# One pair of seven products more in the first half of the two long down linears, with its weight sums made in the mixer

## The chip, the cores and the metric

The kernel runs on one core of a Trainium2 chip. The metric is device microseconds of one execution (a lower number is faster). Of the engines, TensorE (PE in the profile) multiplies, VectorE (DVE) and ScalarE (ACT) prepare its operands and take its results, GpSimd (POOL) and SyncE (SP) issue transfers.

## What is computed

One decoder layer on 256 positions and 16 learned ones put ahead of them, in float32: a SwiGLU network, a mixer (differential attention beside a short gated convolution, merged by gates), a second SwiGLU network, each added to the residual, and a final norm. Cut to what matters here:

```python
D_MODEL, SEQ, N_META, D_FF = 2048, 256, 16, 5632     # D_FF = ((8 * D_MODEL // 3 + 255) // 256) * 256

def swiglu_ffn(h, w_gu, w_down):
    gate, up = jnp.split(h @ w_gu, 2, axis=-1)
    return (jax.nn.silu(gate) * up) @ w_down

s = s + 0.5 * swiglu_ffn(rms_norm(s, norm_ffn1), ffn1_w_gu, ffn1_w_down)
h = rms_norm(s, norm_mix)
q, k, v, b_gate, c_gate, u = jnp.split(h @ w_in, splits, axis=-1)
...                                # attention of q, k, v; convolution of b_gate, c_gate, u; merge
s = s + 0.5 * swiglu_ffn(rms_norm(s, norm_ffn2), ffn2_w_gu, ffn2_w_down)
```

The change lies in the last `@ w_down`; the preparation of its data lies in `h @ w_in`, in the parts k, v, c_gate and u.

## The kernel before

A float32 operand is held as a high and a low part (`wh` and `wl` of a weight: ScalarE casts the high part, VectorE subtracts it from the weight for the low one). One product of two operands is three matmuls into one bank of PSUM: high by high, low by high, high by low.

The second network works on 256 rows as two blocks of 128, in three parts of its hidden width. Two of the parts have 16 chunks of 128 hidden rows: these are the long down linears, each with a first half (`u == 0`, 1024 of the 2048 output columns) and a second. `linear_mix` takes the chunks by pairs. With two row blocks and two column groups of 512, a pair is a 2 x 2 by 2 x 2 block product, and has one of three kinds:

- D: eight products, from two weight tiles of 128x1024.
- S: seven products (a Winograd form of Strassen's scheme), from weight tiles that include four sums of weights. VectorE makes the sums in the linear itself, into the tiles `t13` and `t24` (lines 705, 706, 707).
- P: the same seven products, with the sums read from DRAM (line 693 for `t24`, line 694 for `t13`, 512 KB each, on SP's queue) and three of the four weight blocks (768 KB in place of 1024).

`t13` and `t24` of these linears are the two buffers with the tag "tt". A plan names, by position, the kinds of its pairs, the places at which left-over work of the linear's start is put in, which sums of activations are made when, and the order of the pairs. Eight pairs of seven products each would be 56 products; the plan `DOWN_FIRST` before has six D and two S, so 6 x 8 + 2 x 7 = 62. Sums of the activations (`sp`, ScalarE and VectorE, `sum_of_parts`) are put into the linear by the list `side`, one entry at the end of each pair.

The sums that P pairs read are made earlier, by pieces of half a pair (class `Making`): fetch 512 KB into a tile `mk`, three additions on VectorE, store 512 KB to DRAM (line 339). Most are made in the first network. Five pairs, ten pieces, are made in the mixer by `tick_later`, called once a chunk while v, k, c and u are computed: its step i adds up and stores piece i - 1 and fetches piece i, into the two "tt" buffers in turn. All of these fetches and stores are on GpSimd's queue before.

Around them, in v to u, run the attention steps: TensorE computes scores, VectorE scales them and takes the maximum (lines 960, 964), ScalarE the exponential (line 967), VectorE normalises and takes the difference (lines 971 to 975), TensorE transposes it (`aT`, line 984), ScalarE copies it out (`aB`). Each engine and each queue takes its instructions in the order in which they stand: one that waits holds those behind it.

Of the kernel before, what the change touches and what calls it, by code (L numbers as in the profile page):

```python
# [16 lines left out]
D = 2048  # L17
# [3 lines left out]
F = 5632  # L21
DC = D // P
GC = 4
GW = GC * P
W2 = D // 2
# [12 lines left out]
N_AUX = 3  # L38
# [12 lines left out]
FFN2_MORE = ("DPPPDSPP", (2,), {(4, 1): 5}, ())  # L51
OUT_FIRST = ("DDSDSDSD", (1,), {(1, 1): 2, (3, 1): 4, (5, 1): 6}, ())
OUT = ("DDDDSDSD", (), {(3, 1): 4, (5, 1): 6}, ())
DOWN_FIRST = ("DDDDSDSD", (1,), {(3, 1): 4, (5, 1): 6}, ())
DOWN = ("DDSDSDSD", (), {(1, 1): 2, (3, 1): 4, (5, 1): 6}, ())
DOWN_LAST = ("DDDSDS", (1,), {(2, 1): 3, (4, 1): 5}, ())
AHEAD = 3
# [1 line left out]
TICK_COUNT = 512  # L59
# [11 lines left out]
MADE = [(0, d, p) for d, plan in enumerate(GATE_UNITS) for p, kind in enumerate(plan[0]) if kind == "P"]  # L71
MADE += [(1, u, p) for u in range(F // GW) for p, kind in enumerate(_unit_plan(u)[0]) if kind == "P"]
MADE_LATER = [(0, 0, 1), (0, 0, 3), (1, 1, 5), (1, 2, 1), (1, 3, 1)]
MADE = [m for m in MADE if m not in MADE_LATER]
LATER_TICKS = (TICK_COUNT + 16, TICK_COUNT + 124)


@with_exitstack
def decoder_layer(ctx: ExitStack, tc: tile.TileContext, t, out):
    nc = tc.nc  # L80
# [52 lines left out]
    def load_vectors():  # L133
# [7 lines left out]
        out=mask[:, T - P :],  # L141
        in_=mask[:, T - P :],
# [150 lines left out]
    spare, ticks, last_wl, last_store, last_sum = [], [], [], [], []  # L293
    last_load, ahead_of_split = [], []
    side = []
# [15 lines left out]
        while ahead:  # L311
            ahead.pop(0)[0]()

    made = [[{} for _ in range(n)] for n in (D // GW, F // GW, 2)]

    class Making:

# [1 line left out]
        def __init__(self, n, unit, p, k):  # L319
            self.n, self.unit, self.p, self.k = n, unit, p, k  # L320

        def fetch(self, i, first):
            self.t = early_tile(i)
            if first:
                with tc.issue_after(last_wl[0]):
                    nc.vector.memset(self.t[:, 0, 0:1], 0.0)
            nc.gpsimd.dma_start(out=self.t, in_=t["ffn2_made_of"][self.n, self.k])

        def add(self):
            v = self.t  # L330
# [10 lines left out]
    for n, (f, u, p) in enumerate(MADE):  # L341
        spare.extend(Making(n, made[f][u], p, k) for k in range(2))
    spare_later = [
        Making(len(MADE) + n, made[f][u], p, k) for n, (f, u, p) in enumerate(MADE_LATER) for k in range(2)
    ]

    def tick_later(n):
        n0, n1 = LATER_TICKS
        steps = len(spare_later) + 1
        i = (n - n0) * steps // (n1 - n0)  # L350
        if not n0 <= n < n1 or (n > n0 and i == (n - 1 - n0) * steps // (n1 - n0)):
            return
        if i:
            with tc.issue_after(last_wl[0]):
                spare_later[i - 1].add()
            spare_later[i - 1].store()
        if i < len(spare_later):
            with tc.issue_after(last_store[0]):
                spare_later[i].fetch(N_AUX + i % 2, i < 2)

    def tick():
        ticks.append(0)
# [503 lines left out]
    w_in, w_qb, w_gate, w_out = t["w_in"], t["w_qb"], t["w_gate"], t["w_out"]  # L866
# [182 lines left out]
    for g in range(2):  # L1049
# [7 lines left out]
        if g == 0:  # L1057
# [13 lines left out]
            half = len(units) // 2  # L1071
# [57 lines left out]
    for d in range(D // GW):  # L1129
# [28 lines left out]
        if d < 2:  # L1158
            n = 3 * d
# [39 lines left out]
                out=lo, in0=src, scalar=gain, in1=hi.bitcast(F32), op0=ALU.mult, op1=ALU.subtract  # L1199
            )  # L1200

    def add_mix(plan, a, w, k0, u, by, adds, end):


        v = [[sT[i][u][:, q * GW : (q + 1) * GW] for q in range(2)] for i in range(2)]
        ev = {}

        def scaled(ps, out_, other, op1=ALU.add, by=by):
            nc.vector.scalar_tensor_tensor(out=out_, in0=ps, scalar=by, in1=other, op0=ALU.mult, op1=op1)

        late = []

        def add(out_, in_):
            if adds == "dma":
                late.append(lambda: nc.gpsimd.dma_start(out=out_, in_=in_, accum_op=ALU.add))
            elif adds == "side":
                late.append(lambda: nc.vector.tensor_add(out_, out_, in_))
            else:
                nc.vector.tensor_add(out_, out_, in_)

        def finish_adds():
            if adds == "side":
                side.extend(lambda fs=late[k : k + 2]: [f() for f in fs] for k in (0, 2))
            else:
                for f in late:
                    f()
            end()

        def done(k, ps):
            if k == "1":  # L1230
                ev["a"], ev["b"] = wide([P, 2, GW], "dpa"), wide([P, 2, GW], "dpb")
                nc.scalar.mul(ev["a"][:, 0, :], ps, by)
                add(v[0][0], ev["a"][:, 0, :])
            elif k in "56":
                if k == "6":
                    scaled(ps, ev["a"][:, 1, :], ev["a"][:, 0, :])
                    add(v[1][0], ev["a"][:, 1, :])
                else:
                    ev["p5"] = ps
                if "p5" in ev and (k == "6" or "6" in ev):  # L1240
                    scaled(ev["p5"], ev["b"][:, 0, :], ev["a"][:, 1, :], ALU.subtract)
                    for i in range(2):
                        add(v[i][1], ev["b"][:, 0, :])
            elif k == "7":
                scaled(ps, v[1][0], v[1][0])
                scaled(ps, v[1][1], v[1][1], by=-by)
            else:
                i, q = {"2": (0, 0), "3": (0, 1), "4": (1, 0), "x": (1, 1)}[k]
                scaled(ps, v[i][q], v[i][q])
            ev[k] = True  # L1250
            if all(n in ev for n in "1234567x"):
                pending.append(finish_adds)

        linear_mix(plan, a, w[u], "pd", done, k0)

    def out_done(u):
        def f():
# [58 lines left out]
    w_gu, w_down, w_last = t["ffn2_w_gu"], t["ffn2_w_down"], t["ffn2_w_down_last"]  # L1316
    thirds = [list(range(0, 4)), list(range(4, 8)), list(range(8, ng))]
    for half in thirds:
# [7 lines left out]
        if final:  # L1326
            for q in range(2):
                nc.gpsimd.dma_start(
                    out=gfin[q],
                    in_=t["norm_final"][q * W2 : (q + 1) * W2].rearrange("(o d) -> o d", o=1).to_broadcast([P, W2]),  # L1330
                )
        ma = Mixed(m, 0, True)
        for u in range(2):
# [32 lines left out]
            if final and u == 0:  # L1366
                side.append(lambda: None)
                side.extend(lambda p=p: ma.sum_of_parts(p) for p in (3, 5))
                add_mix(
                    DOWN_LAST, ma, w_down, half[0] * GC, u, 0.5, "side",  # L1370
                    lambda score=score: side.extend(
                        lambda iq=iq: [score(*k) for k in iq] for iq in (((0, 0), (1, 0)), ((0, 1),), ((1, 1),))
                    ),
                )
            elif u == 0:
                side.extend([lambda: None] * 2)
                side.extend(lambda p=p: ma.sum_of_parts(p) for p in (4, 6))
                side.extend((lambda: None, lambda ma=ma: ma.sum_of_parts(2)))
                add_mix(DOWN_FIRST, ma, w_down, half[0] * GC, u, 0.5, "dma", lambda: None)
            elif not final:  # L1380
                add_mix(DOWN, ma, w_down, half[0] * GC, u, 0.5, "dma", lambda: None)
            else:
                linear_tok(ops, w_last, chunks, 0, "pd", down, hold=HOLD, side_at=(1, 2, 3, 4, 5))
# [22 lines left out]
def _laid_out(np, inputs):  # L1406
    a = {k: np.asarray(v) for k, v in inputs.items()}
# [7 lines left out]
    for name in ("ffn1_w_gu", "ffn1_w_down"):  # L1415
        w = a[name][0]
        d[name] = np.stack([_in_fours(w, c) for c in range(0, w.shape[1], GW)])
    w = a["w_in"][0]
# [3 lines left out]
    w = a["w_branch"][0]  # L1422
# [2 lines left out]
    )  # L1425
    d["w_out"] = np.stack([_in_pairs(np, a["w_out"][0], c, c + GW) for c in (0, W2)])
    d["ffn2_w_gu"] = np.stack([_in_pairs(np, a["ffn2_w_gu"][0], c, F + c) for c in range(0, F, GW)])
    ws = [(a["w_gate"][0], D, GW), (a["ffn2_w_gu"][0], F, GW), (a["w_out"][0], GW, W2)]
    d["ffn2_made_of"] = np.stack(
        [  # L1430
            np.stack([_quarter(*ws[f][:2], 2 * p * P, u * ws[f][2] + k * GW // 2, GW // 2) for k in range(2)])
# [38 lines left out]
```

## Time and profile before

| | us |
|---|---|
| runs | 2124.95 (median), 2124.93, 2126.96 |
| profiled execution | 2125.68 |
| its span, first to last instruction | 2123.9 |
| granted clock of TensorE, mean | 0.999 |
| VectorE busy | 1780.8 (84%) |
| ScalarE busy | 1151.4 (54%) |
| GpSimd busy | 164.6 (8%) |
| first long down linear, first half | 1599.98 to 1643.14 |
| the ten pieces made in the mixer | first fetch 896.32, last store 1066.62 |

Times in the trace count from the start of the span. A busy share is a mean over stages with different limits, so a stage is read from its own stretch. The second long down linear begins 245.5 us after the first, at 1845.50.

### The profile page before, as it was taken

What the parts mean: (1) busy time and instruction counts of PE and PEld (TensorE: products, weight loads), DVE (VectorE), ACT (ScalarE), POOL (GpSimd) and SP (SyncE); (2) the same over time, 40 slices, a digit from 0 to 9 for tenths busy, and PEclk for the clock granted to TensorE, in tenths of its full rate; (3) what the DMA queues carried; (4) which work ended last, traced back from release to release, by engine and by line L of the source; (5) the groups of instructions that cost most, each with busy time, mean ns of one, the idle gap of its engine ahead of it and who ended that gap; (6) DMA issues with size and microseconds to landing.
All of it is one profiled execution on the core that took longest, in us unless ns stands there. A gap on an engine that the chain in (4) does not pass through costs nothing.

```text
span 2123.9 us, 33643 instructions
## 1 busy us (share of the span) xinstructions
PE 2112.8 (99%) x13087; PEld 1910.0 (90%) x13087; DVE 1780.8 (84%) x2490; ACT 1151.4 (54%) x1453; POOL 164.6 (8%) x261
## 2 busy tenths in 40 slices
PE   9999999999999999999999999999999999999998
PEld 9999999999999998899998888887888888888887
DVE  8777776677777778978898899999999899998998
ACT  6434443343443445655456565567775567656765
POOL 0111111111121110000000000000000100000000
PEclk9999999999999999999999999999999999999999
DMA  7989999999899885665565665566885988779963
GB/s 301 338 318 330 343 339 330 330 326 337 328 328 335 299 303 195 205 225 199 209 221 200 233 212 192 199 226 238 319 298 193 289 314 305 258 230 313 320 239 139
DMA packets 111328, 576.47 MB, mean 271 GB/s; under 512 B 12992, under 2 KB 13376, under 8 KB 71104
## 3 DMA queue, kind: packets, MB, share of 16 engines
q1 hardware_dynamic: 74160, 444.66, 58.4%
q0 software_dynamic: 36576, 128.99, 17.5%
q8 instruction: 102, 1.67, 0.3%
q10 hardware_dynamic: 432, 0.67, 0.1%
q14 instruction: 58, 0.48, 0.1%
HBM read 506.11 MB, written 63.96 MB: 268 GB/s over the span
## 4 chain that ended last, share of the span: by engine, by line
PE 98%; ACT 0%; DVE 0%; DMA 0%; issue 0%; SPq 0%; ACTq 0%; DVEq 0%
PE pg L666 6%; PE pg L664 6%; PE pg L665 6%; PE pd L447 4%; PE pd L445 4%; PE pu L447 4%; PE pu L446 4%; PE pu L445 4%; PE pg L447 4%; PE pd L446 4%; PE pg L445 4%; PE pg L446 4%; PE pd L664 4%; PE pd L666 4%; PE pd L665 4%; PE g L666 2%
## 5 line engine op out<-in xcount | busy, mean ns | idle before, releaser
L429 ACT CAST wh<-st 128x1024 fp32r<-128x1024 f32 x320 | 335.4, 1049 | 474.3 <-PE pu L446 142.0
L434 DVE TENSOR_TENSOR wl<-st,wh 128x1024 fp32r<-128x1024 f32 x320 | 390.6, 1223 | 211.7 <-ACT wh L429 211.6
L552 DVE TENSOR_TENSOR wl<-st,wh 128x1024 fp32r<-128x1024 f32 (+1 forms) x424 | 453.6, 1085 | 47.4 <-ACT wh L551 43.1
L551 ACT CAST wh<-st 128x1024 fp32r<-128x1024 f32 (+1 forms) x424 | 386.6, 942 | 172.4 <-PE pdx L665 43.2
L551 ACT CAST wh<-t 128x1024 fp32r<-128x1024 f32 x214 | 224.6, 1053 | 204.3 <-DVE t L707 84.1
L552 DVE TENSOR_TENSOR wl<-t,wh 128x1024 fp32r<-128x1024 f32 x214 | 257.9, 1222 | 29.4 <-ACT wh L551 24.2
L447 PE MATMUL pd<-mh,wl 128*128 128x272 f32 x704 | 203.1, 288 | 0.0
L445 PE MATMUL pg<-h,wh 128*128 128x272 f32 x704 | 201.9, 287 | 1.1 <-ACT wh L429 1.1
L445 PE MATMUL pd<-mh,wh 128*128 128x272 f32 x704 | 202.2, 287 | 0.0
L445 PE MATMUL pu<-h,wh 128*128 128x272 f32 x704 | 201.9, 287 | 0.0
L447 PE MATMUL pu<-h,wl 128*128 128x272 f32 x704 | 201.7, 287 | 0.0
L446 PE MATMUL pu<-h,wh 128*128 128x272 f32 x704 | 201.7, 287 | 0.0
L446 PE MATMUL pg<-h,wh 128*128 128x272 f32 x704 | 201.7, 287 | 0.0
L447 PE MATMUL pg<-h,wl 128*128 128x272 f32 x704 | 200.9, 287 | 0.0
L446 PE MATMUL pd<-ml,wh 128*128 128x272 f32 x704 | 200.7, 285 | 0.0
L665 PE MATMUL pg<-wh,h 128*128 128x512 f32 x375 | 146.7, 391 | 0.0
L664 PE MATMUL pg<-wh,h 128*128 128x512 f32 x375 | 146.2, 390 | 0.0
L666 PE MATMUL pg<-wl,h 128*128 128x512 f32 x375 | 145.5, 389 | 0.0
L339 POOL DMA_DIRECT2D made<-mk x118 | 86.1, 729 | 755.1 <-DVE mk L333 605.7
L445 PEld LDWEIGHTS pg<-h,wh 128*128 128x128 f32 x704 | 132.8, 189 | 1.3 <-ACT wh L429 1.3
L446 PEld LDWEIGHTS pd<-ml,wh 128*128 128x128 f32 x704 | 133.5, 190 | 0.0
L446 PEld LDWEIGHTS pg<-h,wh 128*128 128x128 f32 x704 | 132.7, 188 | 0.2 <-DVE h L234 0.2
(392 smaller groups left out, 5101.3 us busy)
## 6 DMA issues: line engine op xcount, KB each, us to landing
st<-in_ffn_w_gu_dram SPq DMA_DIRECT2D x118, 1024.0 KB, 7.3
st<-in_ffn_w_down_dram SPq DMA_DIRECT2D x82, 1024.0 KB, 7.0
mk<-in_ffn_made_of_dram POOLq DMA_DIRECT2D x118, 512.0 KB, 8.3
made<-mk POOLq DMA_DIRECT2D x118, 512.0 KB, 6.4
t<-made SPq DMA_DIRECT2D x118, 512.0 KB, 5.8
st<-in_ffn_w_gu_dram SPq DMA_DIRECT2D x54, 768.0 KB, 6.0
st<-in_w_in_dram SPq DMA_DIRECT2D x32, 1024.0 KB, 5.3
st<-in_w_gate_dram SPq DMA_DIRECT2D x27, 1024.0 KB, 4.8
```

The costliest lines, as they stand in the source:

```text
L339: last_store[:] = [nc.gpsimd.dma_start(out=self.unit[self.p][:, :, cs], in_=self.t).ins]
L429: nc.scalar.copy(out=wh[:, :m, :], in_=sw)
L434: last_wl[:] = [nc.vector.tensor_sub(wl[:, :m, :], sw, wh[:, :m, :].bitcast(F32)).ins]
L445: nc.tensor.matmul(a, wh[:, i, f], act.part(c, 0, t0, t1), start=first, stop=False)
L446: nc.tensor.matmul(a, wh[:, i, f], act.part(c, 1, t0, t1), start=False, stop=False)
L447: nc.tensor.matmul(a, wl[:, i, f], act.part(c, 0, t0, t1), start=False, stop=last)
L551: part_last[:] = [nc.scalar.copy(out=wh, in_=src).ins]
L552: part_last.append(nc.vector.tensor_sub(wl, src, wh.bitcast(F32)).ins)
L664: nc.tensor.matmul(ps[k], hi, wh, start=first, stop=False)
L665: nc.tensor.matmul(ps[k], lo, wh, start=False, stop=False)
L666: nc.tensor.matmul(ps[k], hi, wl, start=False, stop=left[k] == 0)
```

## The change

```diff
-DOWN_FIRST = ("DDDDSDSD", (1,), {(3, 1): 4, (5, 1): 6}, ())
+DOWN_FIRST = ("DDDPDSDP", (1,), {(4, 1): 5}, (0, 1, 3, 4, 5, 6, 7, 2))
...
 MADE_LATER = [(0, 0, 1), (0, 0, 3), (1, 1, 5), (1, 2, 1), (1, 3, 1)]
+MADE_LATER += [(2, 0, k + p) for k in (0, 8) for p in (4, 2)]
...
-LATER_TICKS = (TICK_COUNT + 16, TICK_COUNT + 124)
+LATER_TICKS = (TICK_COUNT + 16, TICK_COUNT + 126)
...
-        def fetch(self, i, first):
+        def fetch(self, i, first, eng=nc.gpsimd):
...
-            nc.gpsimd.dma_start(out=self.t, in_=t["ffn2_made_of"][self.n, self.k])
+            eng.dma_start(out=self.t, in_=t["ffn2_made_of"][self.n, self.k])
...
         if i < len(spare_later):
-            with tc.issue_after(last_store[0]):
-                spare_later[i].fetch(N_AUX + i % 2, i < 2)
+            spare_later[i].fetch(N_AUX + i % 2, i < 2, nc.scalar)
...
-    def add_mix(plan, a, w, k0, u, by, adds, end):
+    def add_mix(plan, a, w, k0, u, by, adds, end, made=None):
...
-        linear_mix(plan, a, w[u], "pd", done, k0)
+        linear_mix(plan, a, w[u], "pd", done, k0, made, True)
...
             elif u == 0:
-                side.extend([lambda: None] * 2)
-                side.extend(lambda p=p: ma.sum_of_parts(p) for p in (4, 6))
-                side.extend((lambda: None, lambda ma=ma: ma.sum_of_parts(2)))
-                add_mix(DOWN_FIRST, ma, w_down, half[0] * GC, u, 0.5, "dma", lambda: None)
+                for p in (None, 4, None, 6, 2):
+                    side.append((lambda: None) if p is None else lambda ma=ma, p=p: ma.sum_of_parts(p))
+                k0 = half[0] * GC
+                ready = {p: made[2][u][k0 // 2 + p] for p in (2, 4)}
+                add_mix(DOWN_FIRST, ma, w_down, k0, u, 0.5, "dma", lambda: None, ready)
...
-    ws = [(a["w_gate"][0], D, GW), (a["ffn2_w_gu"][0], F, GW), (a["w_out"][0], GW, W2)]
+    ws = [(a["w_gate"][0], D, GW), (a["ffn2_w_gu"][0], F, GW), (a["ffn2_w_down"][0], GW, W2), (a["w_in"][0], GW, 3 * W2)]
```

The first half of each long down linear takes its pairs in the order 0 1 3 4 5 6 7 2; pairs 4 and 2 are P, pair 6 is S, the other five are D: 5 x 8 + 3 x 7 = 61 products. The sums for the four P pairs of the two linears are eight more pieces for `tick_later`, eighteen in all, in 110 ticks instead of 108. All eighteen are fetched on ScalarE's queue, without the order behind the last store; a fetch still waits until the store of the piece before it in its buffer has landed. From line 72 on, most line numbers of the changed kernel are larger by one.

In the order of the instructions this stands as follows. ScalarE, at the first attention step (names: `st` a weight as fetched, `vN` values, `mk` a piece, `sc` scores), before:

```order
L429 CAST wh<-st 128x1024 x4
L930 COPY vN_9114<-pv 128x512 x2
L429 CAST wh<-st 128x1024 x2
L967 ACT_TABLE_LOAD
L967 ACTIVATE sc,sm<-sc,mx 128x144 x2
L429 CAST wh<-st 128x1024
L988 COPY aB<-aT 128x128
```

and in the changed kernel:

```order
L429 CAST wh<-st 128x1024 x3
L328 DMA mk<-in_ffn_made_of_dram 128x1024
L429 CAST wh<-st 128x1024
L930 COPY vN_9114<-pv 128x512 x2
L429 CAST wh<-st 128x1024 x2
L328 DMA mk<-in_ffn_made_of_dram 128x1024
L967 ACT_TABLE_LOAD
L967 ACTIVATE sc,sm<-sc,mx 128x144 x2
L429 CAST wh<-st 128x1024
L988 COPY aB<-aT 128x128
L328 DMA mk<-in_ffn_made_of_dram 128x1024
L967 ACTIVATE sc,sm<-sc,mx 128x272 x2
```

Fetches now stand among ScalarE's casts, exponentials and copies; the second one shown, the sixth of the eighteen, is directly ahead of the table load of the first exponential.

VectorE at the same place, before:

```order
L434 TENSOR_TENSOR wl<-st,wh 128x1024
L960 SCALAR_TENSOR_TENSOR sc<-sc_ps,rq,mask 128x144 x2
L434 TENSOR_TENSOR wl<-st,wh 128x1024
L964 TENSOR_REDUCE mx<-sc 128x2
L971 RECIPROCAL rs<-sm 128x2
L972 TENSOR_TENSOR rs<-rs,lam 128x1
```

and in the changed kernel:

```order
L332 TENSOR_TENSOR mk<-mk 128x512
L333 TENSOR_TENSOR mk<-mk 128x256
L334 TENSOR_TENSOR mk<-mk 128x256
L434 TENSOR_TENSOR wl<-st,wh 128x1024
L960 SCALAR_TENSOR_TENSOR sc<-sc_ps,rq,mask 128x144 x2
L434 TENSOR_TENSOR wl<-st,wh 128x1024
L964 TENSOR_REDUCE mx<-sc 128x2
L332 TENSOR_TENSOR mk<-mk 128x512
L333 TENSOR_TENSOR mk<-mk 128x256
L334 TENSOR_TENSOR mk<-mk 128x256
L971 RECIPROCAL rs<-sm 128x2
L972 TENSOR_TENSOR rs<-rs,lam 128x1
```

The first three additions are those whose store the sixth fetch's buffer waits for; they stand one low part ahead of the scaling of the scores. The next three stand between the maximum and the reciprocal.

SP's queue in the first long down linear, before:

```order
L686 DMA st<-in_ffn_w_down_dram 128x2048
L693 DMA t_16748<-made_3547 128x1024
L686 DMA st<-in_ffn_w_down_dram 128x2048 x13
L694 DMA t_17561<-made_3704 128x1024
L686 DMA st<-in_ffn_w_down_dram 128x2048 x2
```

and in the changed kernel:

```order
L693 DMA t_16800<-made_3547 128x1024
L686 DMA st<-in_ffn_w_down_dram 128x2048
L693 DMA t_17024<-made_11598 128x1024
L686 DMA st<-in_ffn_w_down_dram 128x2048
L694 DMA t_17023<-made_11598 128x1024
L686 DMA st<-in_ffn_w_down_dram 128x1536
L686 DMA st<-in_ffn_w_down_dram 128x2048 x3
L686 DMA st<-in_ffn_w_down_dram 128x1536
L686 DMA st<-in_ffn_w_down_dram 128x2048
L693 DMA t_17229<-made_11897 128x1024
L694 DMA t_17228<-made_11897 128x1024
L686 DMA st<-in_ffn_w_down_dram 128x2048 x5
```

The sums of the first P come behind the second and third weight tiles; those of the last P come behind the first weight tile of the second half, and the remaining weights of that half stand behind them.

More of the change, by code (lines that the diff above doesn't have):

```diff
@@ L312, in drain @@
             ahead.pop(0)[0]()
-    made = [[{} for _ in range(n)] for n in (D // GW, F // GW, 2)]
+    made = [[{} for _ in range(n)] for n in (D // GW, F // GW, 2, 2)]
     class Making:
```

## The prediction

> **What bounds the kernel now.** I read the page first, then the list of waits, then stretches and single rows around the two places that the change touches.
>
> ```profile
> PE 2112.8 (99%) x13087; PEld 1910.0 (90%) x13087; DVE 1780.8 (84%) x2490; ACT 1151.4 (54%) x1453; POOL 164.6 (8%) x261
> PE 98%; ACT 0%; DVE 0%; DMA 0%; issue 0%; SPq 0%; ACTq 0%; DVEq 0%
> PE pg L445 <- ACT wh L429: 1.1, 1, 1.1
> PE warm L105 <- DVE ones L99: 1.1, 1, 1.1
> PE pg L664 <- ACT sp L634: 0.7, 1, 0.7
> ```
>
> The first row is the busy time of each engine, the second the chain of work that ended last, by engine; the other three are the waits of TensorE (us in total, times, longest), all but one of 0.2. TensorE is 99% busy, makes up 98% of the chain and waits some 3 us in all. So the time falls only where TensorE has less to do, and rises by whatever it is made to wait. The profiled execution took 2125.68 us (span 2123.9 and 1.78 around it), 0.73 above the 2124.95 median of the runs.
>
> ```profile
> 1622.06 0.39 PE L664 MATMUL pdx<-wh,m 128*128 128x512 f32 x1
> 1622.28 0.39 PE L665 MATMUL pdx<-wh,m 128*128 128x512 f32 x1
> 1622.51 0.39 PE L666 MATMUL pdx<-wl,m 128*128 128x512 f32 x1
> 1622.74 0.39 PE L664 MATMUL pd<-wh,sp 128*128 128x512 f32 x1
> ...
> 1639.74 0.39 PE L664 MATMUL pdx<-wh,m 128*128 128x512 f32 x1
> 1599.98:1643.14 43.16, 43.16 (x196) 35.65 (x194) 40.93 (x59) 23.97 (x28) 0.00 (x0) 1.00 0.56 196
> 1643.14:1683.00 39.86, 39.86 (x177) 33.03 (x176) 35.55 (x40) 22.40 (x24) 3.58 (x4) 1.00 0.88 281
> ```
>
> These are TensorE's matmuls near the end of the first of the two linears that change; below them this linear (1599.98 to 1643.14) and what follows it. In a stretch the columns are length, then busy us of TensorE, its weight loads, VectorE, ScalarE and GpSimd, then clock, DMA share and GB/s. The 0.39 of a row overlaps the next: a product is three matmuls (L664, L665, L666), and its starts are 1622.06 and 1622.74, so it costs 0.68 us at a granted clock of 1.00. VectorE has 2.23 us free in this linear.
>
> **The saving.** Pairs of seven products go from two to three, so each linear has one product less, and there are two such linears: 2 x 0.68 = 1.36 us, or six matmuls of 0.227 us. The Trainium skill's "TensorE: Matmul & The Clock Gate", "Step-by-step: what each phase is for", gives a gap of about 216 ns for 512 columns; by that rule the saving would be about 1.29 us. The trace disagrees by 5% (0.227), and I go by the trace.
>
> **The linear's other engines.** These are the groups of VectorE that change in number.
>
> ```profile
> L705 DVE TENSOR_TENSOR t<-st x48: 1215/1218/1221, 812.1 to 2072.8; 128x1024 f32<-128x1024 f32 x48
> L706 DVE TENSOR_TENSOR t<-t,st x48: 681/684/693, 813.9 to 2074.5; 128x512 f32<-128x512 f32 x48
> L707 DVE TENSOR_TENSOR t<-t,st x48: 682/685/693, 815.6 to 2075.7; 128x512 f32<-128x512 f32 x48
> L551 ACT CAST wh<-t 128x1024 fp32r<-128x1024 f32 x214 | 224.6, 1053 | 204.3 <-DVE t L707 84.1
> 1629.52 0.69 DVE L552 TENSOR_TENSOR wl<-st,wh 128x512 fp32r<-128x512 f32 x1
> 1630.73 1.22 DVE L552 TENSOR_TENSOR wl<-st,wh 128x1024 fp32r<-128x1024 f32 x1
> 1631.86 2.35 DVE L552 TENSOR_TENSOR wl<-t,wh 128x1024 fp32r<-128x1024 f32 x2
> ```
>
> One S pair fewer takes 1.22 + 0.68 + 0.69 = 2.59 us of sums off VectorE; a seven-product pair in place of one with eight adds half a tile and one whole tile of low parts, 0.69 + 1.22 = 1.91. VectorE gets 0.7 us lighter per linear. ScalarE gets one cast of 1.05 and about half of one more, 1.6 us on 23.97 of 43.16: hidden under the matmuls, and if that cover were gone it would be 1.6 us each. The sums of the activations for pairs 4, 6 and 2 are made in both versions and only change place. Each P pair fetches 256 KB less of weights and 1 MB of sums; together 1.5 MB more per linear, some 35 GB/s on 196, below the 281 that the next stretch carries with a fully busy TensorE. I take 0.
>
> The tightest place is the last pair, a P. Its sums are loaded into the two buffers that the S pair two places ahead empties, so SP holds the rest of its queue until VectorE has read them. The first S pair begins at 1622.74 now (the product of sp) and the second 15 products later, at 1632.94; that one had its last low part at 1631.86 + 2.35 = 1634.2, 1.3 after its start. With one S left, a pair of seven later than the first was, it begins at 1622.74 + 7 x 0.68 = 1627.50, and its buffers are free by 1628.8. The loads of such sums landed like this around 1590 to 1700:
>
> ```profile
> DMA to landing us min/median/max: 4.0/6.4/8.9
> L693 SPq DMA_DIRECT2D t<-made x4: 320/326/327, 1673.8 to 1694.4; - x4
> ```
>
> With 0.33 us of issue for each: 1628.8 + 0.7 + 6.4 = 1635.9 at the median, 1638.4 at the longest. TensorE needs the first cast of them at 1639.74 (a product into pdx, the fourth of the last pair, which begins 15 products behind 1627.50, at 1637.70), so the sums at about 1638.7, and the low part 0.5 later. Slack is 2.8 at the median and 0.3 at the longest; with both 1.2-us low parts in a row I bound the cost by 0 and 0.6 per linear, and take 0. The first P, whose buffers the gate linear has read when this one begins (1599.98), has until 1617.30 + 3 x 0.68 = 1619.3, which even a landing of 8.9 leaves 8 us early. The evictions at the end, put behind that pair's low parts, are released by the same VectorE, with 0.7 us less to do. Behind SP's wait stand the second half's weights from its second tile on: issued by 1629.5, they have 13 us until that half begins.
>
> **Making the sums.** Eight more pieces are fetched (512 KB), added up in place on VectorE (L331, L332, L333) and stored, in the stretch from v to u, 892 to about 1081 instead of 1067.
>
> ```profile
> L331 DVE TENSOR_TENSOR mk<-mk x118: 629/684/691, 47.7 to 1064.6; 128x512 f32<-128x512 f32 x118
> L332 DVE TENSOR_TENSOR mk<-mk x118: 404/425/427, 48.5 to 1065.3; 128x256 f32<-128x256 f32 x118
> L333 DVE TENSOR_TENSOR mk<-mk x118: 403/425/427, 49.9 to 1065.8; 128x256 f32<-128x256 f32 x118
> 892.00:932.00 40.00, 39.80 (x305) 38.15 (x304) 28.39 (x45) 23.14 (x31) 3.08 (x5) 1.00 0.61 207
> 932.00:972.00 40.00, 40.00 (x313) 37.31 (x312) 32.14 (x75) 20.23 (x43) 2.52 (x4) 1.00 0.62 228
> 972.00:1012.00 40.00, 40.00 (x318) 37.13 (x317) 31.29 (x77) 21.94 (x55) 2.52 (x4) 1.00 0.58 201
> 1012.00:1052.00 40.00, 40.00 (x329) 38.36 (x328) 38.26 (x91) 20.31 (x41) 2.52 (x4) 1.00 0.53 187
> 1052.00:1092.00 40.00, 40.00 (x332) 39.11 (x331) 33.57 (x65) 20.23 (x37) 1.97 (x3) 1.00 0.68 245
> ```
>
> A piece is 0.68 + 0.43 + 0.43 = 1.54 us of VectorE, eight are 12.3. VectorE is idle 200 - 163.7 = 36.3 us over the five stretches, so on the whole they are hidden. Not so in 1012 to 1052: 1.74 us are free, and the denser schedule puts two more pieces there, 3.1 us. Up to 1.3 us has no room, and it can fall on the chain that the attention steps run through (scores, softmax on ScalarE and VectorE, transpose aT on TensorE). Bounds 0 and 1.3; as VectorE's work can also slide past 1052, where 6.4 is free, I take 0.25. DMA carries 8.4 MB more in 200 us, 42 GB/s on some 214, and stays under the rates seen elsewhere.
>
> **The fetch on ScalarE's queue.** It goes into a buffer whose store, one piece earlier, must have landed, and ScalarE waits for that in order; on GpSimd nothing else waited. Prices: the issue (one other DMA of ScalarE) and the landing of stores (made) and of fetches (mk) from 892 to 1092.
>
> ```profile
> 0.74 0.41 ACTq L124 DMA_DIRECT2D x<-in_x_dram  x1
> L339 POOL DMA_DIRECT2D made<-mk x10: 712/712/721, 910.2 to 1066.6; - x10
> DMA to landing us min/median/max: 3.1/4.5/6.8
> DMA to landing us min/median/max: 4.1/6.3/7.8
> 935.71 1.05 ACT L429 CAST wh<-st 128x1024 fp32r<-128x1024 f32 x1 [1.91 <-PE k L446]
> 936.77 1.28 ACT L967 ACT_TABLE_LOAD   x1
> 938.51 0.42 ACT L967 ACTIVATE sc<-sc,mx 128x144 f32<-128x144 f32 x1 [0.46 <-DVE mx L964]
> 936.34 0.64 DVE L960 SCALAR_TENSOR_TENSOR sc<-sc_ps,rq,mask 128x144 f32<-128x144 f32 x2 [1.29 <-PE sc_ps L957]
> 940.18 0.35 DVE L975 SCALAR_TENSOR_TENSOR sc<-sc,rs 128x128 f32<-128x128 f32 x1
> 941.47 0.33 PE L984 MATMUL aT<-ident,sc 128*128 128x128 f32 x1
> ```
>
> 18 issues x 0.41 = 7.4 us of ScalarE, which is busy 105.9 of these 200: hidden. The waits are the question, and the first attention step is the worst. The sixth fetch stands between the cast of 935.71 and the table load of 936.77, and waits for a store whose adds stand one low part (1.22 us) ahead of the row of 936.34. That row had 1.29 idle before it, so the adds end at 936.34 - 1.29 - 1.22 = 933.8 at the latest, perhaps 0.8 sooner: issue 933.0 to 933.8, landing at the median 937.5 to 938.3, at the extremes 936.1 and 940.6. Behind it come the issue (0.41), the table (1.28) and the chain from exp to the input of aT (938.51 to 940.53, 2.02), and aT is due at 941.47. So TensorE waits from a landing of 941.47 - 3.7 = 937.7 on. At the median that is a wait of between -0.2 and 0.6: I take 0.2, between ends of 0 and 2.9. Later fetches follow their store by a step of about 10 us (189 us in 19 steps) against 4.5 of landing and some 2 us for adds and issue: 3 us of slack, 0.7 at the longest landing, and I take 0 for them. Their cost is bounded by 0 and the 0.4 us of each issue that lands in one of some dozen softmax chains; a fetch then has the rest of a step for its 6.3 before VectorE adds it up. The Trainium skill's "DMA: Bandwidth & Descriptors", "Issuing engines are not separate DMA queues", says that transfers of all issuing engines share the same 16 DMA engines, and that spreading them saves issue time alone. It speaks against any faster fetch; no run here shows it yet, and by it the sum is unchanged. It leaves GpSimd's 0.6 us per fetch as the only relief, on an engine that is 8% busy.
>
> SP's load of the sums for the first gate linear waits for its store, last stored near 1081 now; 6.8 more is 1088, and TensorE starts that linear near 1092 and reads the sums some pairs later. I take 0.
>
> **Sum.** -1.36 + 0.25 + 0.2 = -0.9 us: 2124.8 against the profiled execution's own 2125.68, and 2124.0 against the median of 2124.95. 0.2% of the time, about what a measurement can tell from no change, is 4.25 us; the saving cannot reach that, not even with those 3 us of waits.
>
> **Rivals.**
> - ScalarE held by stores. At the longest landing the first step costs 940.2 - 937.7 = 2.5 us, and each later fetch in a softmax chain about what is over its 0.8 us or so of margin. Decides for slower than before at a sum of waits over 1.36, for a measurable slower over 5.6, or 0.43 for each of 13 fetches. Time 2125 to 2127, and 2130 in the bad case. For it: in-order waiting on a DMA. Against: the 10-us step.
> - VectorE overfull in 1012 to 1052: the 1.3 us with no room, and the same again where the late low parts hold later steps; about 2123.6 + 1.3 to 2.6, 2125 to 2126. Measurably slower only if each of the four or so steps there loses 1.4 us. Against: 6.4 us free behind it.
> - The last P late: landing of 8.9 and then some; 0.6 to 2 us per linear, 2125 to 2128.
> - Nothing hurts: 2123.6. It lies in the forecast's own range.
> - The change does nothing: a product is not dropped. The order has 13015 instructions on TensorE before and 13009 now, so I leave this almost no chance.
> - Faster by more than 4.25 would need a gain that I see no row for.
>
> **Numbers.** Forecast with its small waits, 2123.4 to 2124.9: 0.60. ScalarE held: 0.16 within 0.2%, 0.05 beyond. VectorE: 0.05 within, 0.04 beyond. Last P: 0.05 within, 0.01 beyond. Faster: 0.03. Nothing done: 0.01. So slower 0.10, faster 0.03, same 0.87. The likeliest is 2124.0; the range goes down to 2122.8 (2123.6, less a spread of 0.8 between profiled and median) and up to 2127.6 (2123.6 plus 2.9 at the first step and 1.2 for two late P pairs, the ends that single rows allow), and leaves out about 0.15.
>
> **What would show it.** Six matmuls fewer, and first and second long linear 0.68 shorter (42.5 instead of 43.16). A wait of aT on ScalarE's chain near 941 shows the store wait; sum of TensorE's waits above 5 us, or VectorE at 20 of 20 us near 1030 with TensorE waiting for wl or sc, would make me wrong, as would a wait on casts of t near 1640 or 1885.

## The result, and the profile after

The changed kernel takes 2131.99 us (median of 9 runs), the kernel before 2125.91 beside it: a ratio of 1.0039, 95% interval 1.0030 to 1.0049. By the medians it is slower by 6 us, by the centre of the interval by 8, as two executions at 2140.5 and 2141.2 weigh in it. The prediction was 2124.0 in 2122.8 to 2127.6, with 0.10 for slower. The profiled execution is one of the longer ones: 2140.51, span 2138.7 against 2123.9. One run took 4282.73, twice the others, as did one of the experiment e14 (4282.96); the ratios leave both out.

The page's rows of busy time and of the chain, and the list of TensorE's waits:

```profile
PE 2115.9 (99%) x13081; PEld 1912.1 (89%) x13081; DVE 1788.7 (84%) x2512; ACT 1153.5 (54%) x1457; POOL 164.8 (8%) x259
PE 90%; issue 5%; DMA 3%; DVE 1%; ACT 0%; POOL 0%; SPq 0%; ACTq 0%; POOLq 0%; DVEq 0%
PE aT L984 <- DVE scM L975: 10.1, 5, 6.8
PE pg L664 <- ACT wh L551: 1.1, 1, 1.1
PE pg L445 <- ACT wh L429: 1.1, 1, 1.1
PE warm L106 <- DVE ones L100: 1.1, 1, 1.1
PE aT L984 <- DVE oN L1011: 0.5, 1, 0.5
PE pa L921 <- DVE vz L920: 0.4, 1, 0.4
```

Six matmuls are gone (13087 to 13081), as the change says, and TensorE is still busy longer, 2115.9 against 2112.8: part of its work went slower. Its waits went from 3 to 14 us, and all but 0.4 us of the new ones are on the attention chain, the transposes aT above all. The chain of waits has 3% of DMA and 5% of engines that wait for nothing shown, both at 0 before.

The stretches (length, busy us of TensorE, weight loads, VectorE, ScalarE, GpSimd, then clock, DMA share, GB/s), first from v to u, then the first long linear:

```profile
892.00:932.00 40.00, 39.37 (x299) 37.50 (x298) 28.01 (x46) 20.77 (x27) 2.14 (x3) 1.00 0.73 252
932.00:972.00 40.00, 33.14 (x237) 31.03 (x237) 26.86 (x61) 16.50 (x32) 2.13 (x3) 0.87 0.53 186
972.00:1012.00 40.00, 37.83 (x302) 35.58 (x301) 33.48 (x85) 18.75 (x42) 2.87 (x4) 1.00 0.64 222
1012.00:1052.00 40.00, 38.41 (x298) 34.49 (x297) 33.07 (x80) 20.46 (x53) 2.13 (x3) 1.00 0.69 247
1052.00:1092.00 40.00, 39.84 (x326) 38.44 (x325) 35.23 (x76) 19.75 (x39) 2.85 (x4) 1.00 0.67 237
1616.31:1658.79 42.48, 42.48 (x193) 35.14 (x192) 40.49 (x57) 25.72 (x31) 0.91 (x1) 1.00 0.61 212
```

The long linear is what was forecast to the hundredth: 42.48 us instead of 43.16, 193 matmuls instead of 196, TensorE busy throughout. From its start to the end of the span it is 2138.7 - 1616.31 = 522.4 against 2123.9 - 1599.98 = 523.9: 1.5 us saved. But it starts 16.3 us later. From 892 to 1092 TensorE is busy 188.6 of 200 us, and was busy 199.8: 11.2 of the 16.3 are there. In 932 to 972 the granted clock is 0.87.

The place where most is lost in this execution, first on ScalarE, with the idle time before a row and its cause in brackets:

```profile
933.03 0.33 ACTq L328 DMA_DIRECT2D mk<-in_ffn_made_of_dram  x1
933.49 1.05 ACT L429 CAST wh<-st 128x1024 fp32r<-128x1024 f32 x1 [7.08 <-PE k L447]
934.44 1.07 ACT L930 COPY vN<-pv 128x512 f32<-128x512 f32 x2
935.39 2.00 ACT L429 CAST wh<-st 128x1024 fp32r<-128x1024 f32 x2
945.28 0.33 ACTq L328 DMA_DIRECT2D mk<-in_ffn_made_of_dram  x1
945.65 1.28 ACT L967 ACT_TABLE_LOAD   x1 [8.25 <-issue]
```

The stores on GpSimd, VectorE's waiting row, TensorE, and stretches of 5 us with the columns as above:

```profile
926.36 0.72 POOL L340 DMA_DIRECT2D made<-mk  x1 [11.00 <-DVE mk L334]
938.32 0.71 POOL L340 DMA_DIRECT2D made<-mk  x1 [11.25 <-DVE mk L334]
934.57 1.23 DVE L434 TENSOR_TENSOR wl<-st,wh 128x1024 fp32r<-128x1024 f32 x1 [3.85 <-ACT wh L429]
941.54 0.73 PE L957 MATMUL sc_ps<-kT,qT 64*128 64x272 f32 x4
949.10 0.45 PE L984 MATMUL aT<-ident,sc 128*128 128x128 f32 x1 [6.84 <-DVE scM L975]
940.00:945.00 5.00, 2.27 (x18) 1.69 (x16) 2.55 (x5) 0.00 (x0) 0.71 (x1) 0.96 0.94 337
945.00:950.00 5.00, 0.90 (x4) 0.93 (x5) 2.01 (x8) 3.39 (x7) 0.00 (x0) 0.50 0.47 156
950.00:955.00 5.00, 5.00 (x25) 5.00 (x24) 2.37 (x5) 2.06 (x5) 0.00 (x0) 0.51 0.67 234
955.00:960.00 5.00, 4.97 (x40) 4.50 (x40) 3.04 (x9) 2.33 (x6) 0.00 (x0) 1.00 0.21 80
```

Read from the top. The third store goes out at 926.36, and the fifth fetch, which needs its buffer, is issued by ScalarE at 933.03, 6.7 us later. ScalarE has done nothing for 7.08 us, with its cast behind the fetch. (The bracket names a matmul; a profile of the same kernel further down names the store's landing at this place.) So VectorE waits 3.85 us for the cast, the fourth piece's additions stand behind that, and the fourth store goes out at 938.32, not at 933.0 to 933.8 as the prediction had it. The sixth fetch waits for it until 945.28, 7.0 us after; ScalarE idles 8.25 ahead of the table load of the first exponential, and TensorE 6.84 for the transpose. The clock is at 0.50 for about 10 us, from 2.4 us after TensorE stopped, and matmuls that started 0.125 us apart start 0.227 apart. Some 25 of them start at the slower pace, which is about 2.6 us lost; with the 11.2 that makes 13.8 of the 16.3. The other 2.5 are not placed.

The same holds of every fetch, not only of these two. The third to the eighteenth are issued between 3.1 and 8.3 us after the store of their buffer (918.12 after 909.80, 921.41 after 914.64, up to 1081.15 after 1074.50), each within 0.1 us of that store's landing. So all sixteen had to wait for it.

### The profile page after: what moved, and what is told of

Read it like the earlier page. It is cut to its first block, busy times and chain, and to the rows that moved or that the text cites. A ratio compares the mean times of both kernels' runs of the same rounds, so it can differ in the third digit from the quotient of the medians.

```text
span 2138.7 us, 33731 instructions
## 1 busy us (share of the span) xinstructions
PE 2115.9 (99%) x13081; PEld 1912.1 (89%) x13081; DVE 1788.7 (84%) x2512; ACT 1153.5 (54%) x1457; POOL 164.8 (8%) x259
## 4 chain that ended last, share of the span: by engine, by line
PE 90%; issue 5%; DMA 3%; DVE 1%; ACT 0%; POOL 0%; SPq 0%; ACTq 0%; POOLq 0%; DVEq 0%
PE pg L664 6%; PE pg L665 6%; PE pg L666 6%; PE pd L447 4%; PE pd L445 4%; PE pu L445 4%; PE pu L446 4%; PE pu L447 4%; PE pd L446 4%; PE pg L447 4%; PE pg L445 4%; PE pg L446 4%; PE pd L666 4%; PE pd L665 4%; PE pd L664 4%
## 5 line engine op out<-in xcount | busy, mean ns | idle before, releaser
L552 DVE TENSOR_TENSOR wl<-t,wh 128x1024 fp32r<-128x1024 f32 x218 | 262.7, 1222 | 29.9 <-ACT wh L551 25.7
L340 POOL DMA_DIRECT2D made<-mk x126 | 91.8, 729 | 899.2 <-DVE mk L334 764.2
```

Source lines behind the costliest of these rows:

```text
L340: last_store[:] = [nc.gpsimd.dma_start(out=self.unit[self.p][:, :, cs], in_=self.t).ins]
L552: part_last.append(nc.vector.tensor_sub(wl, src, wh.bitcast(F32)).ins)
```

## Experiments

All times are medians, with the ratio to the kernel before that ran beside them and its 95% interval.

| run | what | us | ratio |
|---|---|---|---|
| e1_gpsimd | fetches on GpSimd, behind the last store | 2144.37 | 1.0090 (1.0077 to 1.0104) |
| e2_making_only | eighteen pieces, old linears | 2132.63 | 1.0038 (1.0024 to 1.0051) |
| e3_linear_only | new linears, ten pieces, sums of other pairs | 2124.28 | 0.9992 (0.9984 to 1.0001) |
| e4_ten_on_scalar | old kernel, ten fetches on ScalarE | 2126.26 | 1.0003 (0.9995 to 1.0012) |
| e5_after_again | the changed kernel | 2136.21 | 1.0049 (1.0034 to 1.0063) |
| e7_made_early | eight pieces in the first network | 2124.35 | 0.9996 (0.9987 to 1.0004) |
| e8_sync | fetches on SP | 2125.59 | 1.0004 (0.9994 to 1.0013) |
| e10_gpsimd_first | fetches on GpSimd, ahead of the store | 2126.55 | 1.0004 (0.9995 to 1.0013) |
| e11_short_stores | eight stores of a quarter | 2129.44 | 1.0020 (1.0011 to 1.0029) |
| e12_same_order_whole | its control, whole stores | 2133.10 | 1.0037 (1.0024 to 1.0050) |
| e13_two_later | fetch two chunks later | 2132.20 | 1.0039 (1.0026 to 1.0052) |
| e14_made_early_again | as e7_made_early | 2123.75 | 0.9992 (0.9983 to 1.0002) |

**Which half of the change costs.** One run keeps the eighteen pieces with the old linears, one the new linears with the old ten pieces, one the old kernel with its ten fetches moved to ScalarE.

```diff
# e2_making_only
-DOWN_FIRST = ("DDDPDSDP", (1,), {(4, 1): 5}, (0, 1, 3, 4, 5, 6, 7, 2))
+DOWN_FIRST = ("DDDDSDSD", (1,), {(3, 1): 4, (5, 1): 6}, ())
# e3_linear_only (and the ten fetches on GpSimd, as before)
-MADE_LATER += [(2, 0, k + p) for k in (0, 8) for p in (4, 2)]
-                ready = {p: made[2][u][k0 // 2 + p] for p in (2, 4)}
+                ready = {2: made[1][2][1], 4: made[1][3][1]}
# e4_ten_on_scalar, against the kernel before
-            with tc.issue_after(last_store[0]):
-                spare_later[i].fetch(N_AUX + i % 2, i < 2)
+            spare_later[i].fetch(N_AUX + i % 2, i < 2, nc.scalar)
```

> The long down linears are those of the kernel before (62 products, no P pair); all eighteen pieces are made as in the changed kernel, and the eight new ones are not used. Theory (the loss is all in v to u, the linear itself saves its 1.36 us): 1.4 us slower than the changed kernel, 2131 to 2135. Rival (the linear with P pairs costs some of the loss, by late sums or late evictions): faster than the changed kernel by 1 us or more, 2126 to 2131.

> The new linears without the eight new pieces: ten pieces on GpSimd's queue as before, and the P pairs of the long down linears read the sums of other pairs (so the products of these pairs are of other weights; times and traffic are the same). Theory: 1.4 us faster than before, within 1 us: 2123.5 to 2125.5. Rival (late sums of the last P or the evictions behind it): 0 to 3 us slower than before, with waits of TensorE in the long linears.

> The kernel before with one part of the change alone: its ten pieces are fetched on ScalarE's queue, without the order behind the last store; no new piece, old linears. Theory (a fetch holds ScalarE only where the store two pieces back has not landed, and ten pieces in 108 ticks leave it 11 us and more): same as before within 1 us, 2124 to 2127. Rival (the issue on ScalarE's queue itself, 0.33 us among the exponentials, or the lost order, is what costs): 2 to 5 us slower than before, 2128 to 2131.

The loss is there with the making alone (1.0038 against 1.0039), and absent from the linears alone, whose profile has the same stretch as the changed kernel's:

```profile
1600.50:1642.98 42.48, 42.48 (x193) 35.12 (x192) 39.91 (x57) 25.67 (x31) 0.40 (x1) 1.00 0.61 212
```

From its start to the span's end are 2123.1 - 1600.50 = 522.6 us, 1.3 less than before; the median is 1.25 below that of before. That is the size that six matmuls should have, though the interval of the ratio just includes 1. Making without use was expected to be 1.4 slower than the changed kernel; the scatter of the changed kernel (2131 to 2141) hides such a difference. Ten fetches on ScalarE cost 0.7 us, within noise: the issue itself, 0.33 us each, is not the loss. The reason given for it was not right, though: its eight fetches that need a buffer went out 3.2 to 7.4 us after their stores, each when the store landed. ScalarE waited there too, but of that only 0.5 us reached TensorE.

**Who waits.** The first test put the fetches back on GpSimd as they were.

```diff
# e1_gpsimd
-            spare_later[i].fetch(N_AUX + i % 2, i < 2, nc.scalar)
+            with tc.issue_after(last_store[0]):
+                spare_later[i].fetch(N_AUX + i % 2, i < 2)
```

> The changed kernel with one part undone: all eighteen pieces are fetched on GpSimd's queue again, behind the last store, as before. Theory (ScalarE is held by a fetch that waits for a store, above all ahead of the first exponential, and TensorE waits for the transposes behind it): the waits of TensorE for aT, 10 us in the changed kernel's profile, fall below 2, and the time falls by 5 to 8 us to 2124 to 2127. Rival (the eight more pieces load VectorE and the DMA engines, whoever fetches): within 2 us of the changed kernel, 2130 to 2133. Second rival (fetches on GpSimd come so late that VectorE, in order, waits for a piece to add up): the wait moves to VectorE's additions, 2127 to 2131.

It is the slowest of all, and my theory's number was wrong by 17 us. What the second rival describes is what happened, 13 us above its own upper end. Its waits of TensorE, VectorE's wait for pieces, and two pieces on GpSimd's queue:

```profile
PE pa L922 <- DVE vz L921: 4.9, 1, 4.9
PE aT L985 <- DVE scM L976: 4.8, 3, 2.6
PE u L448 <- DVE wl L435: 2.7, 1, 2.7
DVE mk L332 <- DMA mk<-in_ffn_made_of_dram: 25.5, 10, 7.0
1081.37 0.71 POOL L340 DMA_DIRECT2D made<-mk  x1 [10.49 <-DVE mk L334]
1082.01 0.62 POOL L328 DMA_DIRECT2D mk<-in_ffn_made_of_dram  x1
1092.87 0.72 POOL L340 DMA_DIRECT2D made<-mk  x1 [10.25 <-DVE oN L1042]
```

Each fetch stands right behind a store that waits for the additions of the piece before: one piece at a time, 11.5 us each (1081.37 to 1092.87), more than the 10 that eighteen pieces leave. Here VectorE is held, 25.5 us, and with it everything that it gives to TensorE. So the theory was put differently: the round trip through two buffers is too long for the pace, some engine waits for it, and the cost depends on what is queued behind that wait. Two placements test this, with the same pieces, additions and stores:

```diff
# e10_gpsimd_first: the fetch ahead of the additions and the store, on GpSimd
+        if i < len(spare_later):
+            spare_later[i].fetch(N_AUX + i % 2, i < 2)
         if i:
             with tc.issue_after(last_wl[0]):
                 spare_later[i - 1].add()
             spare_later[i - 1].store()
-        if i < len(spare_later):
-            spare_later[i].fetch(N_AUX + i % 2, i < 2, nc.scalar)
# e8_sync
-            spare_later[i].fetch(N_AUX + i % 2, i < 2, nc.scalar)
+            spare_later[i].fetch(N_AUX + i % 2, i < 2, nc.sync)
```

> All eighteen pieces in v to u, fetched on GpSimd's queue, but each fetch stands ahead of the store of the piece before it, and not behind: two pieces can be on their way at once. Theory (with fetches on GpSimd behind the last store, one piece at a time takes some 11 us, and VectorE waits 25 us for pieces; two at a time need 14 to 17 per two, and only GpSimd waits for stores): TensorE's waits under 3 us, 2124 to 2128. Rival (the additions and traffic of eight more pieces are too much by themselves): 2130 to 2134. Second rival (GpSimd, held by a fetch, brings the next store late, and VectorE still waits for pieces): 2128 to 2138 with DVE mk waits of 10 us or more.

> The changed kernel with its eighteen fetches on SP's queue, in the same places of the order. With fetches ahead of the stores on GpSimd, GpSimd waited 82 us for landed stores, up to 6.9 at a time, and TensorE lost little. Theory (the wait costs by what is queued behind it): behind SP's wait stand the weights, fetched up to three tiles ahead; a tile feeds TensorE about 6 us, so waits of 7 us are mostly covered: 2125 to 2131, faster than the changed kernel. Rival (late weights reach the casts and so TensorE): 2132 to 2140, with TensorE's waits on casts and low parts in place of those on aT.

Waits for a store that has not landed, of GpSimd in the first and of SP in the second; with VectorE's waits for pieces, and on SP a wait of TensorE. Below them are the stretch of the first attention steps and the one that VectorE fills most:

```profile
POOL mk L328 <- DMA made<-mk: 81.9, 19, 6.9
DVE mk L332 <- DMA mk<-in_ffn_made_of_dram: 6.5, 4, 3.4
932.00:972.00 40.00, 40.00 (x313) 37.31 (x313) 34.65 (x82) 20.43 (x42) 5.18 (x8) 1.00 0.73 263
1012.00:1052.00 40.00, 39.90 (x327) 38.20 (x328) 38.21 (x93) 20.25 (x41) 4.38 (x7) 1.00 0.67 234
```

```profile
SPq L328 <- DMA made<-mk: 76.8, 16, 8.8
DVE mk L332 <- DMA mk<-in_ffn_made_of_dram: 5.1, 3, 3.7
PE yt L1042 <- DVE oN L1041: 0.9, 1, 0.9
932.00:972.00 40.00, 40.00 (x313) 37.31 (x312) 34.49 (x82) 20.53 (x42) 2.86 (x4) 1.00 0.78 276
1012.00:1052.00 40.00, 39.90 (x328) 38.20 (x327) 38.21 (x93) 20.71 (x41) 2.14 (x3) 1.00 0.68 241
```

GpSimd waits 82 us and SP 77, up to 8.8 at a time, and TensorE is nearly as busy in these stretches as in the kernel before (40.00 and 39.90 of 40, against 40.00 in both). Both kernels take what the one before takes, with eighteen pieces. The additions on VectorE and the traffic are the same as in the changed kernel, so they are not what makes it slower; what left ScalarE is the fetch, its issue and its wait. The issue alone cost nothing clear of noise with ten pieces. On SP the weights stand behind the fetch, and no wait of TensorE on a cast or a low part is above 0.6 us there. In both, 1052 to 1092 still has TensorE busy only 38.83 and 38.54, which is about the saving of the linears. On SP, VectorE stands idle 3.7 us there for a late piece, until 1068.05, is then busy without a break from 1072 to 1088, and TensorE waits 0.9 us for its oN and 0.6 for a low part. On GpSimd the same rows have 3.4, 0.6 and 0.6. So the round trip through two buffers still costs something there, by way of VectorE.

**The landing.** If ScalarE's wait is for a landing, a shorter store must help.

```diff
# e11_short_stores (for the eight new pieces, which come first in e11 and e12; P pairs read sums of other pairs)
-            last_store[:] = [nc.gpsimd.dma_start(out=self.unit[self.p][:, :, cs], in_=self.t).ins]
+            last_store[:] = [nc.gpsimd.dma_start(out=self.unit[self.p][:, 0:1, cs], in_=self.t[:, 0:1, :]).ins]
```

> The changed kernel with its fetches on ScalarE, but the eight new pieces come first in v to u and store a quarter of their sums (128 of 512 KB); the P pairs of the long linears read the sums of other pairs instead, so three quarters of those sums are left out and these products are of other weights. Additions on VectorE and fetches are unchanged. Theory (ScalarE's wait for a store's landing is the loss): stores land 2 to 3 us sooner, the waits for aT up to the middle of the stretch mostly go, 2125 to 2129. Rival (the additions on VectorE): 2131 to 2133 as in the changed kernel.

> The control of the run with short stores: eight new pieces first, the P pairs of the long linears read the sums of other pairs, but all stores whole (512 KB). Theory (the landing of stores is the loss): 2 to 6 us slower than with short stores, 2131 to 2136. Rival (the order of the pieces, not the length of the stores, made that run faster): within 1 us of it, 2128 to 2130.

2129.44 against 2133.10 of its control: 3.7 us of the 8 go with the eight short stores. The two ran in different sets, and their intervals just touch (1.0011 to 1.0029 and 1.0024 to 1.0050). Nor is it the landing alone. The eight stores landed after 2.2 to 7.6 us, median 3.6, against 3.1 to 7.1, median 4.2, in the control, so 0.6 us sooner by the median; and a short store waits only for the first of the three additions (line 332), and so goes out about 1 us earlier. Both shorten ScalarE's wait, and the run does not separate them. TensorE's row for aT went from 4.0 us in five waits (control) to

```profile
PE aT L987 <- DVE scM L978: 3.1, 3, 2.6
```

which is only a part of it. Over 892 to 1092 TensorE is busy 196.6 of 200 us against 194.0 in the control, whose profile is one of the better of its runs (2129.2 of span).

**A miss, and a repeat.** Moving each fetch two chunks later in the code was to show the same from the other side.

```diff
# e13_two_later
-            spare_later[i].fetch(N_AUX + i % 2, i < 2, nc.scalar)
+            late_at.append(n + 2)        # fetched by the call of chunk n + 2, for i > 1
```

> The changed kernel with each fetch still on ScalarE's queue, but two chunks later in the order of the instructions (from the third piece on), 3 to 5 us in which the store ahead can land. Theory (ScalarE waits for the landing): the waits for aT fall under 3 us, but pieces come later to VectorE, which then waits more than the 5 us of the changed kernel; 2126 to 2131. Rival (the issue of a DMA among the exponentials costs by itself): no change from 2131 to 2136.

Its instructions stand in the same order on ScalarE, VectorE and GpSimd as those of the changed kernel: the line that asks for a fetch does not alone decide where it stands in the queue. So this is the changed kernel again, at 2132.20, and the question was not tested. But its profile shows an execution nearer to the middle of the runs (2134.31) than the one read above:

```profile
PE aT L993 <- DVE scM L984: 5.5, 5, 2.9
932.00:972.00 40.00, 38.48 (x300) 35.84 (x298) 34.11 (x80) 19.14 (x41) 2.85 (x4) 1.00 0.67 245
972.00:1012.00 40.00, 37.06 (x281) 34.42 (x279) 27.33 (x69) 15.68 (x33) 2.14 (x3) 0.96 0.56 190
```

Here the first attention step costs 1.50 us, and the longest wait, 2.94, is at 982, at a later step. From 892 to 1092 TensorE is idle 7.7 us, of which 6 lie outside the first attention step. Again each of the sixteen fetches goes out when its store lands, 3.1 to 8.7 us after it. So the long wait at 942 belongs to the longest executions; the usual loss is made of smaller ones along the whole stretch.

The changed kernel itself came out as before:

> The changed kernel once more, beside the others of this set. Eight of its nine earlier runs lay at 2131 to 2141, its profiled one at 2140.5. Theory (two buffers and a round trip of store and fetch of 14 us or more; whichever engine issues the fetch waits): 2131 to 2133, TensorE's waits for aT of 3 to 6 us in place of 10, and ScalarE idle for some us ahead of fetches with no other cause shown. Rival (VectorE's additions are the load): VectorE 20 of 20 us busy where TensorE waits.

Its runs went from 2131.05 (clock 0.999) to 2140.49 (0.996), against 2131 to 2133 expected. In the profiled one the two rows of ScalarE at the first attention step, its waits for stores before casts in all, and TensorE's for aT are

```profile
932.30 1.05 ACT L429 CAST wh<-st 128x1024 fp32r<-128x1024 f32 x1 [5.60 <-DMA made<-mk]
942.37 1.28 ACT L967 ACT_TABLE_LOAD   x1 [5.45 <-DMA made<-mk]
ACT wh L429 <- DMA made<-mk: 16.4, 3, 6.4
PE aT L984 <- DVE scM L975: 7.2, 4, 4.1
932.00:972.00 40.00, 35.85 (x261) 33.59 (x259) 29.88 (x68) 18.45 (x37) 2.14 (x3) 0.91 0.58 210
```

Here the profile names the cause that stood as TensorE's matmul and as "issue" in the brackets above: the store's landing. VectorE is not full where TensorE waits for aT (29.88 of 40 us in 932 to 972), so the rival of this run falls there. It is full around 1087 (5.00 of 5 us from 1085 to 1090), where TensorE waits 1.7 us for oN; for that part it stands.

**A version without the wait.** The eight pieces go to the first network, among its 108, with its five buffers.

```diff
# e7_made_early, e14_made_early_again (fetches on GpSimd as before)
-MADE_LATER += [(2, 0, k + p) for k in (0, 8) for p in (4, 2)]
+MADE += [(2, 0, k + p) for k in (0, 8) for p in (4, 2)]
```

> The new linears, but their eight pieces are made in the first network with the others (116 pieces in 512 ticks instead of 108, five buffers, GpSimd's queue); v to u makes ten pieces as before. Theory: the loss in v to u is gone and the linears' saving stays: 2123.5 to 2126. Rival (the first network's DMA share of 0.9 has no room for 8 MB more): 2127 to 2132, with new waits of TensorE before 890.

> The version with the eight pieces made in the first network once more, for a narrower interval. Theory (the linears save two products, nothing else changes): 1.4 us faster than before, 0.9990 to 0.9998 of it. Rival (hidden, or lost again in the first network): the same as before.

2124.35 and 2123.75, 0.97 and 1.18 below the kernel before in the same sets. Both intervals still include 1, so it is shown faster than the changed kernel, and as fast as before or a little faster. TensorE's waits are back to some 2 us:

```profile
PE warm L106 <- DVE ones L100: 1.1, 1, 1.1
PE pg L665 <- ACT sp L635: 0.6, 1, 0.6
PE pg L446 <- ACT wh L430: 0.4, 1, 0.4
PE qb_ps L890 <- ACT u2x L750: 0.2, 1, 0.2
```

## Why the prediction was wrong

- **The saving: right.** 0.68 us per linear, to the hundredth in the stretch; 1.3 to 1.5 us from the first long linear to the end. The Trainium skill's "TensorE: Matmul & The Clock Gate", "Step-by-step: what each phase is for", gave 1.29 by its gap of 216 ns; the 0.227 of the trace held: three matmuls fewer made the linear 0.68 us shorter.
- **The linears' other engines: right.** VectorE 40.49 of 42.48 (0.44 less, 0.7 forecast), ScalarE 25.72 (1.75 more, 1.6 forecast), no wait of TensorE for the last P's sums.
- **The additions on VectorE, 0.25 with ends of 0 and 1.3: harmless where they were feared.** With the fetches on GpSimd ahead of the stores or on SP, 1012 to 1052 has TensorE at 39.90 of 40. What is lost there, 1.2 to 1.5 us, is behind 1052, where VectorE had been idle for a late piece.
- **Later fetches, 0 by a step of 10 us and 3 us of slack: the step that failed.** The working took a fetch to follow its store by a whole step, so that the store had landed when ScalarE came to the fetch. In the profile this holds for none of the sixteen: each went out 3.1 to 8.3 us after the issue of its store, at the landing, and not 10 us after it. So there was no slack at any of them. In the execution at 2134, 6 of the 7.7 idle us of TensorE are outside the first attention step. Why the fetches stand so early in ScalarE's queue was not found; moving the line that asks for them by two chunks did not change it.
- **The first attention step, 0.2 with ends of 0 and 2.9: right in its mechanism, 1.50 us in the execution at 2134, but 6.84 in the one at 2140, and 2.6 of slow clock behind it.** The working took the sixth fetch by itself against the old times. But the fifth had already held ScalarE for 7 us, and so delayed, through cast and low part, the very additions whose store the sixth waits for: the store went out at 938.3, not 933.8. The wait feeds itself, ScalarE to VectorE to GpSimd's store and back to ScalarE. The landing was 6.7 to 7.0 where I took the median of 4.5.
- **The rival "ScalarE held by stores": it is what happened**, at 2131 to 2141 where I gave 2125 to 2127 and 2130 in the bad case. Its chance beyond 0.2% was 0.05. Its price left out the clock. That its mechanism was on the list, with a small chance and too low a price, is not a forecast of it.
- **"GpSimd's 0.6 us per fetch as the only relief": wrong the other way.** The order of the kernel before, with eighteen pieces, costs 19 us. The queue did matter. The Trainium skill's "DMA: Bandwidth & Descriptors", "Issuing engines are not separate DMA queues", says that transfers share the same engines whoever starts them; nothing here speaks against that, but the engine that starts one also waits for its buffer, and that decided between 2144, 2132 and 2126.
- **Two sums.** The top of the range is 2123.6 + 2.9 + 1.2 = 2127.7 by its own terms, not 2127.6, and 10 - 4.5 - 2 leaves 3.5 us of slack (1.2 at the longest landing), not 3 and 0.7. Neither changes the outcome.

That the loss in the changed kernel comes from the fetches on ScalarE is shown by the runs that move them to GpSimd and SP, which take what the kernel before takes; that it is the wait for the landing and not the issue, by the rows of the repeat that name it and by the ten fetches that cost nothing clear of noise. That the half clock adds some 3 us in the longest executions is read from one profile and agrees with the clock of the runs (0.996 to 0.997 at 2140, 0.998 to 0.999 at 2131 to 2136). Why some executions have the long wait and others not was not tried.

## What to carry to other kernels

A transfer that must wait for its buffer holds everything behind it on the engine that issues it: put it where what stands behind can wait, and price it with all waits in a row, not one at a time against the old times. Before making more of something through the same buffers, work out the round trip (landing of the store, landing of the fetch, work between), and read from the order of the instructions how far each fetch stands behind its store; the mean distance of the pieces does not say it. A gain of 0.06% on the bound engine is lost to one such wait.

## What was unexpected of the hardware

Around a wait of 6.84 us TensorE's granted clock was 0.50 for 10.2 us: from 2.4 us after TensorE stopped until 5.8 after it went on. Behind a wait of 4.1 us (the repeat) it was 0.50 for 6.8 us, and behind waits of 2.65 (short stores), 2.94 (fetches two chunks later), 1.68 (making alone) and 1.46 (the repeat, at 1087) for 3.4 us each. So in these six places the slow time came in steps of about 3.4 us. The length of the wait alone does not decide: 1.46 and 1.68 us brought the clock down in two runs, and 1.66 in the control left it at 1.00. The Trainium skill's "TensorE: Matmul & The Clock Gate", "What's actually happening", has half the clock after an idle window of about 3.4 us; the 0.50 agrees, and the drops at waits of 1.5 to 2.9 us came with less idle time than that figure.

Stores of 512 KB from GpSimd's queue landed after 3.1 to 8.3 us in the changed kernel's profile (median 5.7, against 4.5 before), but with a median of 4.6 in the repeat's, and up to 9.3 there. So the landing of one store scatters by a factor of three in one stretch of one execution, and a rise with twice the pieces is not shown.
